# A four-layer decoder trunk on one core: transposes of four head pairs moved from TensorE to VectorE and GpSimd, with edges and one low part reordered

## The chip, the core and the metric

The kernel runs on one core of a Trainium2 chip. A core has five engines that run beside each other: TensorE (PE; its weight loads are listed as PEld), VectorE (DVE), ScalarE (ACT), GpSimd (POOL) and SyncE (SP), which here issues the loads from memory. The metric is the device time of one execution in microseconds, as the median of several runs.

## What is computed

Four layers, each a token mixer and then an MLP with squared ReLU, over one residual stream of 256 tokens by 1024. The mixers are differential attention (layers 0 and 3), block-sparse attention (layer 1, whose one block of 256 makes it plain causal attention here) and sliding-window attention with sinks (layer 2).

```python
for i in range(DEPTH):                       # 4
    a = rms_norm(h, attn_norm_g[i])
    if i % 3 == 0:   y = diff_attention(a, ...)      # 8 heads of 128, (softmax1 - lam * softmax2) v
    elif i % 3 == 1: y = moba_attention(a, ...)      # 16 heads of 64, softmax(q k) v
    else:            y = swa_sink_attention(a, ...)
    h = h + y
    h = h + (max(rms_norm(h, mlp_norm_g[i]) @ w_up, 0) ** 2) @ w_down
return rms_norm(h, final_norm_g)
```

## The kernel before

Every fp32 product is made of two or three faster ones: a matrix is split into a high part, rounded by ScalarE (`whi`, line 188), and a low part, the rest, made by VectorE (`wlo`, line 189). Weights come in pieces of 128x2048 (`raw`, 1 MB each) that SyncE loads up to five pieces ahead of their use (`take`, `FAR`) and that are split two pieces ahead (`LOOK`), each in two halves; the split buffers hold three pieces. A layer uses its pieces in this order: twelve for the input projection (`p_in`), four for the output projection (`p_d`, `p_e` in layer 1), sixteen for the up projection, sixteen for the down projection.

The input projection of layers 0, 1 and 3 makes six groups of 512 columns. For layer 1 they are queries and keys of head pairs 0-1, 2-3, then values, then queries and keys of pairs 4-5 and 6-7, then values. Between the matmuls of these groups stand the attention's steps; a hand-written list, `plan`, says after which group each step is issued: QK (turn queries and keys, `p_qk`, and split them into `qhl` and `kpadh`, `kpadl`), SC (scores `p_s`, then numerators `e`: a mask and row minimum on VectorE, line 466, an exponential on ScalarE, line 469), TR (turn the numerators, `p_t`, and copy them out of PSUM, `et`), AV (product with the values, `p_av`) and, in layers 0 and 3, OUT (turn the results, `p_o`, and split them into `oo`).

In layer 1 a step covers one head pair (two heads of 64, called head 0 to 7 here). `head_block` makes the numerators of both heads in one tile of 128x768, divides them by their sums (line 560) and yields; `next` then runs TR: `transposed` makes six 128x128 transposes on TensorE against an identity (line 131) and two copies by ScalarE (line 485) into one of four `et` tiles, taken in turn; `next` again runs AV: eight matmuls into `p_av`, whose high and low parts go into `oo`. PSUM tiles named "wk" (`p_s`, `p_t`, `p_qk`, `p_av`, `p_o` and others) share four banks in turn.

In layers 0 and 3 `diff_head` combines the two softmaxes (line 518) and `diff_pair` makes the product of two heads, normalises it on VectorE (line 537, tile `o`), and after a `yield` turns it and makes its high part on ScalarE (line 547) and its low part on VectorE (line 548). `ahead` holds one edge that `stage` adds: the first half of one low weight part comes behind line 537 of the last pair.

The order on each engine is made by a scheduler; `TURNS` corrects it on TensorE. Per layer it lists edges such as `(("p_t", 18), ("p_d", 61))`: the matmul number 18 of those that write `p_t` in this layer comes behind number 61 of those that write `p_d`. `behind` makes such an edge between two instructions of one engine; it orders them and waits for nothing. All matmuls have the helper's line 128 in the profile and all transposes line 131, so they are told apart by their tiles.

At the end of the kernel the same way of turning that the change brings into layer 1 exists already for the residual stream: `turn_stream` has VectorE turn squares of 32x32 (line 864) and GpSimd copy them to their places (line 869), in 64 copies of 32x128.

Of the kernel before, what the change touches and what calls it, by code (L numbers as in the profile page):

```python
# [15 lines left out]
OP = mybir.AluOpType  # L16
# [3 lines left out]
P = 128  # L20
# [10 lines left out]
FAR = 5  # L31
WARM = 10
RAW = 4

# [17 lines left out]
        (("p_s", 4), ("p_in", 119)),  # L52
        (("p_s", 42), ("p_d", 41)),
        (("p_d", 150), ("p_d", 161)),
        (("p_o", 12), ("p_d", 126)),
        (("p_t", 18), ("p_d", 61)),
        (("p_av", 18), ("p_t", 23)),
        (("p_av", 21), ("p_d", 84)),
        (("p_s", 7), ("p_in", 116)),
        (("p_s", 12), ("p_in", 164)),  # L60
        (("p_s", 13), ("p_in", 168)),
        (("p_s", 16), ("p_in", 168)),
    ),
    1: (
        (("p_s", 0), ("p_in", 83)),
# [3 lines left out]
        (("p_s", 1), ("p_in", 85)),  # L69
        (("p_s", 13), ("p_in", 133)),  # L70
        (("p_s", 37), ("p_in", 277)),
        (("p_t", 42), ("p_d", 26)),
        (("p_s", 4), ("p_in", 85)),
        (("p_s", 16), ("p_in", 133)),
        (("p_s", 40), ("p_in", 277)),
        (("p_s", 42), ("p_d", 0)),
        (("p_d", 27), ("p_t", 47)),
        (("p_s", 18), ("p_in", 144)),
    ),
    2: (  # L80
# [21 lines left out]
        (("p_s", 4), ("p_in", 85)),  # L102
        (("p_s", 42), ("p_d", 41)),
        (("p_d", 150), ("p_d", 161)),
        (("p_o", 12), ("p_d", 126)),
        (("p_t", 18), ("p_d", 61)),
        (("p_av", 18), ("p_t", 23)),
        (("p_av", 21), ("p_d", 84)),
    ),
}  # L110
# [2 lines left out]
def f(ap):  # L113
    return ap.bitcast(F32)
# [31 lines left out]
def trunk(ctx: ExitStack, tc: tile.TileContext, xT, gains, lams, swa_row, fng, weights, out):  # L146
    nc = tc.nc
    V, A, G, T = nc.vector, nc.scalar, nc.gpsimd, Numbered(nc.tensor)
# [6 lines left out]
    def bank(tag, name):  # L155
        return ps.tile([P, 512], F32, tag=tag, name=name, bufs=4)

    def room(j, shape, name, dt=F32):

        return sb.tile(shape, dt, tag=f"slot{j}", name=name, bufs=1)  # L160


    fetched, staged, highs = [], [], []
# [15 lines left out]
    def stage(w=1024, first=None):  # L179
        i = len(staged)  # L180
        raw = fetched[i]
        hi = sb.tile([P, 2048], F32R, tag="whi", name=f"whi{i}", bufs=LOOK + 1)
        lo = sb.tile([P, 2048], F32R, tag="wlo", name=f"wlo{i}", bufs=LOOK + 1)
        for h in range(2048 // w):
            if first:
                first()
            s = slice(h * w, (h + 1) * w)
            high = A.activation(hi[:, s], raw[:, s], AF.Copy)  # L188
            low = V.tensor_tensor(lo[:, s], raw[:, s], f(hi[:, s]), op=OP.subtract)  # L189
            if (i, h) in ahead:  # L190
                behind(tc, low.ins, ahead[i, h])
        highs.append(high.ins)
        staged.append((hi, lo))

    used = [0]
# [10 lines left out]
    def r3(n):  # L206
        return lambda t: t.rearrange("p (a b) -> p a b", a=n)
# [39 lines left out]
    causal = cst.tile([P, 3, P], F32, name="causal")  # L247
# [193 lines left out]
    scored, turned = [0], [0]  # L441
# [36 lines left out]
    def transposed(es):  # L478
        turned[0] += 1
        ts = room((6, 7, 12, 13)[turned[0] % 4], [P, 2, 3 * P], "et")  # L480
        for i, e in reversed(list(enumerate(es))):
            p = bank("wk", "p_t")
            for j in range(3):
                T.transpose(p[:, P * j:P * j + P], e[:, P * j:P * j + P], ident)
            A.activation(ts[:, i], p[:, :3 * P], AF.Copy)
        return [ts[:, i] for i in range(len(es))]

    def times_v(o, et, v):

        T.matmul(o(0), et[:, 0:P], v(0), start=True, stop=True)  # L490
        T.matmul(o(1), et[:, P:2 * P], v(0), start=True, stop=False)
        T.matmul(o(1), et[:, 2 * P:3 * P], v(1), start=False, stop=True)
# [31 lines left out]
    def diff_pair(slot, ets, v, el, b):  # L524

        p = bank("wk", "p_av")
        for c in range(2):
            times_v(lambda t, c=c: p[:, S * c + P * t:S * c + P * t + P], ets[c], v[c])
        ss = tiny.tile([P, 2 * NT], F32, tag="ss", name="ss")
        for t in range(2 * NT):  # L530
            junk = sb.tile([P, P], F32, tag="junk", name="junk", bufs=1)
            A.activation(junk, p[:, P * t:P * t + P], AF.Square, accum_out=ss[:, t:t + 1])
        V.scalar_tensor_tensor(ss, ss, 1.0 / P, el, op0=OP.mult, op1=OP.add)
        y = tiny.tile([P, 2 * NT], F32, tag="ry", name="ry")
        rsqrt(y, ss, 2 * NT)
        o = sb.tile([P, 2 * NT, P], F32, tag="o", name="o")
        made = V.tensor_tensor(o, p.rearrange("p (t m) -> p t m", m=P), y[:, :, None].to_broadcast([P, 2 * NT, P]),
                               op=OP.mult)
        if b == 6:

            ahead[used[0] + 4, 0] = made.ins
        yield
        p = bank("wk", "p_o")
        for t in range(2 * NT):
            T.transpose(p[:, P * t:P * t + P], o[:, t, :], ident)
        both, gain = part(b, 2), sg[:, slot:slot + 1]
        A.activation(both[:, :, 0], r3(2)(p), AF.Copy, scale=gain)
        V.scalar_tensor_tensor(both[:, :, 1], r3(2)(p), gain, f(both[:, :, 0]), op0=OP.mult, op1=OP.subtract)
        yield [both[:, 0], both[:, 1]]

    def head_block(parts, q, k, v, mask, sinks, b):

        _, both_e, l = scores(q, k, mask, sinks)

        rl = tiny.tile([P, 2, 3], F32, tag="rl3", name="rl3")
        l = l.rearrange("p (c t) -> p c t", c=2)
        V.reciprocal(rl[:, :, 0:2], l)
        V.reciprocal(rl[:, :, 2:3], l[:, :, 1:2])
        e = both_e.rearrange("p c (j m) -> p c j m", j=3)
        V.tensor_tensor(e, e, rl[:, :, :, None].to_broadcast([P, 2, 3, P]), op=OP.mult)  # L560
        es = [both_e[:, c] for c in range(2)]
        yield
        ets = transposed(es)
        yield
        p = bank("wk", "p_av")
        for m, cols in ((0, slice(0, S)), (1, slice(P, S))):
            for c in range(2):
                r = slice(HD * c, HD * c + HD)
                T.matmul(p[r, cols], v(m)[:, r], ets[c][:, S * m:S * m + S - P * m], start=(m == 0), stop=(m == 1),
                         skip_group_check=True)  # L570
        both = part(b)
        A.activation(both[:, 0], p[:, :S], AF.Copy)
        V.tensor_tensor(both[:, 1], p[:, :S], f(both[:, 0]), op=OP.subtract)
        parts.append(both)
# [42 lines left out]
    def mixer_layer(i, n):  # L617
        mixer, slot = i % 3, i // 3
        r = norm_factor(n, i == 0, mixer != 1 and i < 3)
        parts = []  # L620
        kpad = new_keys()
        if mixer == 2:
# [15 lines left out]
            for c in range(4):  # L638
                p = proj(n, (256, 1), False, first)
# [24 lines left out]
        else:  # L664
            v = [room(8 + j, [P, NT, 512], f"v{j}") for j in range(2)]
            vdone = 0
            qk, qs, heads, pairs, ets, els = {}, {}, {}, {}, {}, {}
# [6 lines left out]
            def vh(h):  # L674
                return lambda m: v[h // 4][:, m, P * (h % 4):P * (h % 4) + P]

            def SC(h):
                q, k = [x[:, h % 2] for x in qs[h // 2]], [x[:, h % 2] for x in kpad]
                if mixer == 0:
                    if h % 2 == 0:  # L680
                        els[h // 2] = tiny.tile([P, 2 * NT], F32, tag="el", name="el")
                    heads[h] = diff_head(slot, q, k, els[h // 2][:, NT * (h % 2):NT * (h % 2) + NT])
                else:
                    heads[h] = head_block(parts, q, k, vh(h), causal, None, h)
                next(heads[h])

            def TR(h):
                ets[h] = next(heads[h])

            def AV(h):  # L690
                if mixer:
# [9 lines left out]
            def LAM(_):  # L701
                if i == 0:
                    lambdas()

            order = (0, 1, "v", 2, 3, "v") if mixer else (0, 1, "v", 2, "v", 3)
            plan = [[], [], [(QK, 0), (LAM, 0), (SC, 0)], [(SC, 1)], [(TR, 0), (QK, 1), (SC, 2)], [(TR, 1), (SC, 3)],
                    [(TR, 2)], [(TR, 3)], [(QK, 2), (SC, 4)], [(AV, 0), (AV, 1), (AV, 2), (AV, 3), (SC, 5)],
                    [(TR, 4), (QK, 3), (SC, 6)], [(TR, 5), (SC, 7)],
                    [(TR, 6), (TR, 7), (AV, 4), (AV, 5), (AV, 6), (AV, 7)]]
            if mixer == 0:  # L710
                plan[6:8] = [[(TR, 2), (AV, 0)], [(TR, 3), (AV, 1)]]
# [3 lines left out]
            for at, c in enumerate(order):  # L715
                p = proj(n, (512, 2), at == 0, [lambda do=do, x=x: do(x) for do, x in plan[2 * at]])
# [249 lines left out]
    for i in range(DEPTH):  # L966
        T.layer = i
        parts, rest = mixer_layer(i, n)
# [98 lines left out]
```

## Time and profile before

| | us |
|---|---|
| median of 3 runs | 1133.9 (1132.7 to 1134.74) |
| the profiled execution | 1133.25 |
| its span, first to last instruction | 1131.4 |
| TensorE busy | 1123.7 |
| VectorE busy | 831.9 |
| ScalarE busy | 657.1 |
| GpSimd busy | 56.8 |

A row of the timeline has the start in us from the span's start, the time from the first start to the last end of a run of equal instructions, engine, line, operation, output and inputs, shape, and their number; in brackets stands idle time before it with what ended it. Starts of TensorE's instructions are exact and their ends are modelled, so two neighbouring rows overlap: the distance of their starts is what an instruction cost. In a view by groups the numbers behind the bar are the busy time in us, the mean of one in ns, and the idle time before.

### The profile page before, as it was taken

How to read it: one execution, taken by the hardware profiler on the slowest of the kernel's cores; microseconds unless marked ns; L12 is line 12 of the kernel's file. 1: busy time of each engine (PE TensorE's matmuls, PEld its weight loads, DVE VectorE, ACT ScalarE, POOL GpSimd, SP SyncE). 2: the span in 40 equal slices, each digit the busy share in tenths (PEclk: the TensorE clock that was granted, in tenths of full speed). 3: DMA queues.
4: the chain of work that ended last, by engine and by line, in shares of the span. 5: the costliest groups of instructions: out<-in, count | busy, mean ns of one | idle time of the engine just before them, and what ended most of it. 6: DMA issues, size and time to landing. Idle time of an engine off the chain costs nothing.

```text
span 1131.4 us, 17032 instructions
## 1 busy us (share of the span) xinstructions
PE 1123.7 (99%) x6522; PEld 979.5 (87%) x6522; DVE 831.9 (74%) x1599; ACT 657.1 (58%) x1195; POOL 56.8 (5%) x113
## 2 busy tenths in 40 slices
PE   9999999999999999999999999999999999999997
PEld 7889888888888888888899998888888889888886
DVE  8888977656676698766569888775568788878453
ACT  7766666544476665654446866554446776665342
POOL 2000000000100000000000000000010000002800
PEclk9999999999999999999999999999999999999999
DMA  8643565555544346555563346555554444654551
GB/s 328 203 149 113 178 203 194 196 197 187 171 164 149 115 156 219 193 200 189 196 211 112 113 150 218 191 187 186 186 187 149 150 149 150 213 195 169 186 186 38
DMA packets 30465, 198.66 MB, mean 176 GB/s; under 512 B 3504, under 2 KB 5040, under 8 KB 7216
## 3 DMA queue, kind: packets, MB, share of 16 engines
q1 hardware_dynamic: 30096, 197.09, 50.7%
q8 instruction: 51, 0.84, 0.3%
q10 hardware_dynamic: 288, 0.49, 0.1%
q14 instruction: 30, 0.25, 0.1%
HBM read 196.52 MB, written 1.05 MB: 175 GB/s over the span
## 4 chain that ended last, share of the span: by engine, by line
PE 97%; DMA 1%; issue 0%; SPq 0%; DVE 0%; ACT 0%; POOLq 0%; POOL 0%; DVEq 0%
PE p_up L128 31%; PE p_down L128 24%; PE p_in L128 19%; PE p_last L128 7%; PE p_d L128 7%; PE p_s L128 3%; PE p_av L128 2%; PE p_t L131 1%; PE p_qk L131 1%; DMA raw<-in_weights 1%; PE p_e L128 1%; PE p_o L131 0%; SPq L220 0%; SPq L174 0%; DVE wlo L189 0%
## 5 line engine op out<-in xcount | busy, mean ns | idle before, releaser
L189 DVE TENSOR_TENSOR wlo<-raw,whi 128x1024 fp32r<-128x1024 f32 (+1 forms) x374 | 449.0, 1215 | 187.9 <-ACT whi L188 187.5
L188 ACT ACTIVATE whi<-raw 128x1024 fp32r<-128x1024 f32 (+1 forms) x374 | 383.8, 1045 | 197.7 <-issue 112.9
L128 PE MATMUL p_up<-hg,whi 128*128 128x512 f32 x1024 | 355.3, 394 | 0.0
L128 PE MATMUL p_up<-hg,wlo 128*128 128x256 f32 x1024 | 283.0, 277 | 0.0
L128 PE MATMUL p_down<-uu,whi 128*128 128x512 f32 x768 | 266.4, 394 | 0.0
L128 PEld LDWEIGHTS p_up<-hg,whi 128*128 128x128 f32 x1024 | 191.8, 188 | 44.1
L128 PE MATMUL p_in<-whi,hg 128*128 128x512 f32 (+1 forms) x736 | 212.7, 371 | 0.1
L128 PE MATMUL p_down<-uu,wlo 128*128 128x256 f32 x768 | 212.7, 277 | 0.0
L128 PEld LDWEIGHTS p_up<-hg,wlo 128*128 128x128 f32 x1024 | 192.2, 188 | 0.4
L128 PEld LDWEIGHTS p_down<-uu,whi 128*128 128x128 f32 x768 | 144.0, 188 | 33.5
L128 PEld LDWEIGHTS p_in<-whi,hg 128*128 128x128 f32 x736 | 132.5, 189 | 23.5 <-DVE hg L345 0.8
L128 PEld LDWEIGHTS p_down<-uu,wlo 128*128 128x128 f32 x768 | 144.1, 188 | 0.0
L128 PE MATMUL p_in<-wlo,hg 128*128 128x512 f32 (+1 forms) x368 | 130.1, 368 | 0.3 <-DVE wlo L189 0.3
L834 ACT ACTIVATE uu<-u 128x512 fp32r<-128x512 f32 x64 | 40.5, 632 | 80.4 <-DVE u L832 80.4
L128 PE MATMUL p_d<-oo,whi 128*128 128x256 f32 (+1 forms) x416 | 85.4, 296 | 0.0
L128 PE MATMUL p_last<-whi,uu 128*128 128x512 f32 (+1 forms) x264 | 79.4, 383 | 0.0
L128 PEld LDWEIGHTS p_in<-wlo,hg 128*128 128x128 f32 x368 | 68.8, 189 | 11.6 <-DVE wlo L189 0.8
L754 ACT ACTIVATE cross<-p_up 128x256 f32<-128x256 f32 x128 | 48.0, 375 | 35.5 <-PE p_up L128 34.2
L128 PEld LDWEIGHTS p_d<-oo,whi 128*128 128x128 f32 x416 | 66.5, 190 | 2.1 <-issue 0.2
L344 ACT ACTIVATE hg<-hT,gn 128x256 fp32r<-128x256 f32 x64 | 31.4, 504 | 61.0 <-DVE hT L767 60.9
L469 ACT ACTIVATE e<-ns,nm 128x128 f32<-128x128 f32 (+1 forms) x128 | 56.8, 446 | 13.3 <-DVE nm L466 13.2
L128 PE MATMUL p_d<-oo,wlo 128*128 128x256 f32 x224 | 63.7, 285 | 0.0
(170 smaller groups left out, 1106.3 us busy)
## 6 DMA issues: line engine op xcount, KB each, us to landing
raw<-in_weights SPq DMA_DIRECT2D x181, 1024.0 KB, 4.9
raw<-in_weights SPq DMA_DIRECT2D x8, 256.0 KB, 4.7
raw<-in_weights SPq DMA_DIRECT2D x4, 512.0 KB, 7.6
hT<-in_xT SPq DMA_DIRECT2D x8, 128.0 KB, 4.6
bias<-in_swa_row SPq DMA_DIRECT2D x1, 512.0 KB, 4.4
grow<-in_fng SPq DMA_DIRECT2D x1, 512.0 KB, 3.7
lv<-in_lams SPq DMA_DIRECT2D x1, 256.0 KB, 6.6
out<-given ACTq DMA_DIRECT2D x1, 256.0 KB, 2.7
```

What stands on the lines that cost most here:

```text
L128: return self.keep(out.tensor.name.rstrip("_0123456789"), self.engine.matmul(out, *args, **kw))
L131: return self.keep(out.tensor.name.rstrip("_0123456789"), self.engine.transpose(out, *args, **kw))
L188: high = A.activation(hi[:, s], raw[:, s], AF.Copy)
L189: low = V.tensor_tensor(lo[:, s], raw[:, s], f(hi[:, s]), op=OP.subtract)
L344: A.activation(both[:, 0], h, AF.Copy, scale=g)
L469: A.activation(e[:, s], ns[:, s], AF.Exp, bias=nm[:, t:t + 1], scale=-1.0, accum_out=l[:, t:t + 1])
L754: A.activation(cross, p[:, S:], AF.Copy)
L834: A.activation(both[:, :, 0], r3(2)(u), AF.Copy)
```

## The change

In layer 1 head pairs 0, 1, 2 and 4 (`ASIDE`) no longer use `transposed`. `turned_aside` has VectorE turn every 32x32 square of the 128x768 numerators in one instruction into a new tile (`squares`, in slots 16 and 17, which otherwise serve the end of the kernel), and GpSimd copy the squares to their places in `et`: sixteen copies of 32 partitions by 192 columns for a pair, 64 in all. For pairs 0 to 2 this is issued directly behind the scores; for pair 4 it is moved in `plan` one step forward, behind the products of pairs 0 to 3, whose first `et` tile it takes over.

`lows` keeps the last low half of each weight piece, and the second half of the one that had the edge behind line 537 is now behind the low part of the last results (before line 548), which puts this low part one weight half forward.

In `TURNS` layers 0 and 3 have three edges with other numbers (p_t 18 behind p_d 65 instead of 61; p_av 18 behind p_d 79 instead of p_t 23; p_o 12 behind p_d 125 instead of 126), layer 0 one edge more (p_s 9 behind p_in 115), and layer 1 two edges renumbered for the smaller count of `p_t` and moved: the last pair's transposes come behind p_d 31 instead of 26.

In the built order of instructions this is what moves. On TensorE 24 transposes are gone from layer 1; the scores of pairs 2 and 3 stand together behind matmul 143 and 144 of `p_in` (before, the first stood behind 131 and the second behind 144); the other moves are those of the edges named, four matmuls or fewer each, and in layer 0 matmul p_in 115 stands before p_s 3. On ScalarE eight copies are gone; in layer 1 the second half of the keys for pairs 2 and 3 comes behind two weight roundings; in layers 0 and 3 the copy of head 6 stands between two roundings. On VectorE four turns are added. SyncE's order of loads is the same.

```diff
+ASIDE = (0, 1, 2, 4)
...
-        (("p_o", 12), ("p_d", 126)),
-        (("p_t", 18), ("p_d", 61)),
-        (("p_av", 18), ("p_t", 23)),
+        (("p_o", 12), ("p_d", 125)),
+        (("p_t", 18), ("p_d", 65)),
+        (("p_av", 18), ("p_d", 79)),
...
+        (("p_s", 9), ("p_in", 115)),
...
-        (("p_t", 42), ("p_d", 26)),
+        (("p_t", 18), ("p_d", 31)),
...
-        (("p_d", 27), ("p_t", 47)),
+        (("p_d", 32), ("p_t", 23)),
...
         highs.append(high.ins)
+        lows.append(low.ins)
...
+    def turned_aside(pair_e, h):
+
+        turned[0] += 1
+        ts = room((6, 7, 12, 13)[turned[0] % 4], [P, 2, 3 * P], "et")
+        z = room(16 + h % 2, [P, 2, 3 * P], "squares")
+        V.transpose(z.rearrange("p c m -> p (c m)"), pair_e.rearrange("p c m -> p (c m)"))
+        to, at = (x.rearrange("p c (j i m) -> p (c j) i m", j=3, m=32) for x in (ts, z))
+        for g in range(4):
+            for i in range(4):
+                G.tensor_copy(to[32 * i:32 * i + 32, :, g, :], at[32 * g:32 * g + 32, :, i, :])
+        return [ts[:, i] for i in range(2)]
...
-            ahead[used[0] + 4, 0] = made.ins
+            then = used[0] + 4
+            ahead[then, 0] = made.ins
...
-        V.scalar_tensor_tensor(both[:, :, 1], r3(2)(p), gain, f(both[:, :, 0]), op0=OP.mult, op1=OP.subtract)
+        made = V.scalar_tensor_tensor(both[:, :, 1], r3(2)(p), gain, f(both[:, :, 0]), op0=OP.mult, op1=OP.subtract)
+        if b == 6:
+            behind(tc, lows[then], made.ins)
...
-    def head_block(parts, q, k, v, mask, sinks, b):
+    def head_block(parts, q, k, v, mask, sinks, b, aside=False):
...
-        ets = transposed(es)
+        ets = turned_aside(both_e, b) if aside else transposed(es)
...
-                    heads[h] = head_block(parts, q, k, vh(h), causal, None, h)
+                    heads[h] = head_block(parts, q, k, vh(h), causal, None, h, h in ASIDE)
                 next(heads[h])
+                if mixer and h in ASIDE and h < 4:
+                    next(heads[h])
 
             def TR(h):
-                ets[h] = next(heads[h])
+                if not (mixer and h in ASIDE and h < 4):
+                    ets[h] = next(heads[h])
...
-                    [(TR, 2)], [(TR, 3)], [(QK, 2), (SC, 4)], [(AV, 0), (AV, 1), (AV, 2), (AV, 3), (SC, 5)],
-                    [(TR, 4), (QK, 3), (SC, 6)], [(TR, 5), (SC, 7)],
+                    [(TR, 2)], [(TR, 3)], [(QK, 2), (SC, 4)], [(AV, 0), (AV, 1), (AV, 2), (AV, 3), (TR, 4), (SC, 5)],
+                    [(QK, 3), (SC, 6)], [(TR, 5), (SC, 7)],
```

More of the change, by code (lines that the diff above doesn't have):

```diff
@@ L104 @@
         (("p_d", 150), ("p_d", 161)),
-        (("p_o", 12), ("p_d", 126)),
-        (("p_t", 18), ("p_d", 61)),
-        (("p_av", 18), ("p_t", 23)),
+        (("p_o", 12), ("p_d", 125)),
+        (("p_t", 18), ("p_d", 65)),
+        (("p_av", 18), ("p_d", 79)),
         (("p_av", 21), ("p_d", 84)),
@@ L160, in room @@
         return sb.tile(shape, dt, tag=f"slot{j}", name=name, bufs=1)
-    fetched, staged, highs = [], [], []
+    fetched, staged, highs, lows = [], [], [], []
     ahead = {}
```

## The prediction

> **What bounds the kernel now.** I read the page first, then busy time by stretch, then TensorE's timeline where the change touches it, and last the timelines of the engines that feed it.
>
> ```profile
> span 1131.4 us, 17032 instructions
> PE 1123.7 (99%) x6522; PEld 979.5 (87%) x6522; DVE 831.9 (74%) x1599; ACT 657.1 (58%) x1195; POOL 56.8 (5%) x113
> ...
> PE 97%; DMA 1%; issue 0%; SPq 0%; DVE 0%; ACT 0%; POOLq 0%; POOL 0%; DVEq 0%
> ...
> 327.00:400.00 73.00, 72.87 (x424) 61.05 (x423) 51.83 (x123) 51.63 (x117) 0.00 (x0) 1.00 0.42 145
> ```
>
> TensorE (PE) works 99% of the span, and 97% of the chain of waits is its own. The last row is the attention of the second layer (layer 1) (columns: PE, PEld, DVE, ACT, POOL, clock, DMA share, GB/s): PE 72.87 of 73 us, VectorE (DVE) 51.8, ScalarE (ACT) 51.6, GpSimd (POOL) nothing, clock 1.00, DMA at 0.42. So the time is the sum of what TensorE issues plus its short stalls. What leaves TensorE is won, unless its replacement arrives late; what is put on VectorE and GpSimd costs nothing until TensorE waits for it. "Busy" hides short stalls, since a matmul's end is modelled; I find them as the distance between starts against the usual step (0.228 us for 512 columns, 0.12 for 256, 0.11 for a transpose).
>
> **The change part by part.** *Transposes taken from TensorE.* Heads 0, 1, 2 and 4 of the second layer (each a pair) lose six transposes each.
>
> ```profile
> 327.02 0.82 PE L131 MATMUL p_t<-ident,e 128*128 128x128 f32 x6
> 327.67 1.04 PE L131 MATMUL p_qk<-ident,qk 128*128 128x128 f32 x8
> ...
> 361.98 2.82 PE L128 MATMUL p_av<-et,v 128*64 128x256 f32 x32
> ```
>
> Six transposes hold the next instruction back 327.67 - 327.02 = 0.65 us. Four such blocks go: 4 x 0.65 = **-2.60 us**. Eight copies out of PSUM leave ScalarE too, which wins nothing by itself.
>
> *The last pair's transposes.* In the built order they stand three output-projection matmuls later.
>
> ```profile
> 386.10 0.96 DVE L560 TENSOR_TENSOR e<-e,rl 128x768 f32<-128x768 f32 x1
> ...
> 386.80 0.28 PE L128 MATMUL p_d<-oo,wlo 128*128 128x256 f32 x1
> 387.21 0.85 PE L131 MATMUL p_t<-ident,e 128*128 128x128 f32 x6
> 387.99 2.82 PE L128 MATMUL p_av<-et,v 128*64 128x256 f32 x32
> ```
>
> From 386.80 to 387.21 are 0.41 us where a step is 0.12: 0.29 us of waiting for the numerators, ready at 387.06. The chain that makes them starts from TensorE's scores, so it moves forward with TensorE; three more matmuls (0.12 + 0.23 + 0.12 = 0.47 us) cover the hole: **-0.29**.
>
> *Edges in the first and the fourth layer (layers 0 and 3).*
>
> ```profile
> 100.15 0.75 DVE L518 SCALAR_TENSOR_TENSOR e<-e,c 128x128 f32<-128x128 f32 x2
> ...
> 100.26 0.40 PE L128 MATMUL p_d<-oo,whi 128*128 128x256 f32 x2
> 100.65 0.74 PE L131 MATMUL p_t<-ident,e 128*128 128x128 f32 x3
> 101.35 0.40 PE L128 MATMUL p_d<-oo,whi 128*128 128x256 f32 x2
> ...
> 930.35 0.40 PE L128 MATMUL p_d<-oo,whi 128*128 128x256 f32 x2
> ...
> 931.42 0.40 PE L128 MATMUL p_d<-oo,whi 128*128 128x256 f32 x2
> ```
>
> From 100.26 to 101.35 are 1.09 us for three matmuls and three transposes (3 x 0.12 + 3 x 0.11 = 0.69): 0.40 lost, waiting for the numerators that VectorE ends at 100.90; in the fourth layer 1.07 - 0.69 = 0.38. Four matmuls (0.48 us) now stand ahead, so the transposes come at 100.98: **-0.40 and -0.38**. The copy of this result on ScalarE now stands between two weight roundings, and the product that reads it (p_av 18) is moved behind four matmuls.
>
> ```profile
> 101.74 0.48 ACT L485 ACTIVATE et<-p_t 128x384 f32<-128x384 f32 x1
> 102.11 2.00 ACT L188 ACTIVATE whi<-raw 128x1024 fp32r<-128x1024 f32 x2
> ...
> 103.22 0.83 PE L128 MATMUL p_av<-v,et 128*128 128x128 f32 x6
> ```
>
> One rounding of 1.0 us from 101.74 and the copy behind it end at 103.2; the product comes at 103.22 - 0.40 + 0.48 = 103.3: 0.1 us to spare, no cost.
>
> ```profile
> 110.29 2.35 DVE L189 TENSOR_TENSOR wlo<-raw,whi 128x1024 fp32r<-128x1024 f32 x2
> 112.56 0.74 DVE L548 SCALAR_TENSOR_TENSOR oo<-p_o,gn,oo 128x512 fp32r<-128x512 f32 x1
> ...
> 113.15 0.59 PE L128 MATMUL p_d<-oo,whi 128*128 128x256 f32 x2
> 113.58 0.28 PE L128 MATMUL p_d<-oo,wlo 128*128 128x256 f32 x1
> ...
> 943.22 0.58 PE L128 MATMUL p_d<-oo,whi 128*128 128x256 f32 x2
> 943.64 0.28 PE L128 MATMUL p_d<-oo,wlo 128*128 128x256 f32 x1
> ```
>
> The low part of the last results (L548) waits behind two 1.2 us weight operations and ends at 113.30; the matmuls there take 0.43 and 0.42 us for two steps of 0.12: 0.19 and 0.18 us of stall. With one weight operation moved behind it, and its transposes one matmul earlier, it ends over 0.5 us sooner: **-0.19 and -0.18**. The weight half behind it is for the up projection, which reads it several microseconds later.
>
> ```profile
> 34.52 0.69 DVE L615 TENSOR_TENSOR kpadl<-p_qk,kpadh 64x512 fp32r<-64x512 f32 x1
> ...
> 34.84 0.40 PE L128 MATMUL p_in<-whi,hg 128*128 128x512 f32 x1
> 35.35 0.47 PE L128 MATMUL p_s<-kpadh,qhl 128*128 128x512 f32 x1
> ```
>
> The new edge in the first layer puts one ready 512-column matmul (p_in 115) into the hole before 35.35, where TensorE waits 0.28 us for the keys: **-0.23**.
>
> *What the new road costs.* Four VectorE turns of 128x768, 64 GpSimd copies of 32x192.
>
> ```profile
> 323.27 0.95 DVE L560 TENSOR_TENSOR e<-e,rl 128x768 f32<-128x768 f32 x1
> ...
> 364.43 0.96 DVE L560 TENSOR_TENSOR e<-e,rl 128x768 f32<-128x768 f32 x1
> ...
> 1042.75 1.29 DVE L864 STREAM_TRANSPOSE squares<-hT 128x512 f32<-128x512 f32 x2
> ...
> L869 POOL COPY res<-squares x64: 279/288/1360, 1039.6 to 1072.2; 32x128 f32<-32x128 f32 x64
> 1039.64 33.74 POOL L869 COPY res<-squares 32x128 f32<-32x128 f32 x64 [80.37 <-DVE squares L864]
> ...
> L189 DVE TENSOR_TENSOR wlo<-raw,whi x11: 1216/1221/1226, 324.7 to 359.4; 128x1024 fp32r<-128x1024 f32 x11
> L189 DVE TENSOR_TENSOR wlo<-raw,whi x14: 1185/1276/1314, 1039.4 to 1073.1; 128x1024 fp32r<-128x1024 f32 x14
> ...
> L235 POOL MEMSET ones<- 128x128 f32 x1 | 0.2, 204 | 0.3 <-POOLq L1056 0.3
> L250 POOL MEMSET causal<- 128x384 f32 x1 | 0.4, 422 | 0.0
> ```
>
> A turn: 0.64 us for 512 columns, so about 0.96 for 768 (L560 has the same shape and takes 0.95). VectorE is idle for 21 of the 73 us; weights are split two pieces ahead; four turns stay hidden. A copy of 32x128 takes 0.288 us undisturbed and, with its issue, 0.33; up to 1.36 when VectorE runs a weight split beside it, and the split grows from 1221 to 1276 ns. For 192 columns: not below 0.33, not above 1.5 x 0.33 = 0.49; the memsets grow by 0.85 ns a column, so I take 0.33 + 0.055 = 0.385.
>
> Are they in time? Head 0's turn ends near 325.3 (behind L560 at 323.27 and a mask operation). The first product to read the copies is the block at 361.98, by then 3 x 0.65 = 1.95 earlier, and head 2's part lies 1.4 us inside: 361.4. That leaves 36.1 us for 48 copies, **0.75 us each**. In this time VectorE does twelve splits, three normalisations and one rotation of two SBUF inputs, some 12 x 1.22 + 3 x 0.95 + 1.4 = 19 us; free are 17 us, or 44 copies at 0.385, and as in the older stretch about one slips in at each of the blocking operations (19 more): 63 places for 48. At 0.49 it is 35 + 19 = 54. Head 4's sixteen have from about 365 to 385, 1.2 us each. So: hidden, and if the cover fails the product block waits one for one.
>
> The thin place is the scores of heads 2 and 3, which now stand together behind the "v" projection: the second half of the keys is rounded only after both halves of a weight piece on ScalarE.
>
> ```profile
> 331.49 2.01 ACT L188 ACTIVATE whi<-raw 128x1024 fp32r<-128x1024 f32 x2 [0.40 <-PE p_in L128]
> ...
> 335.10 0.82 PE L131 MATMUL p_t<-ident,e 128*128 128x128 f32 x6
> ```
>
> That piece starts 0.65 earlier, at 330.84, and ends at 332.85, the keys at about 333.4; TensorE reaches the scores at 335.10 - 0.65 - 1.04 (six score matmuls moved behind) = 333.4. The keys' low half follows in much the same way. No slack: between 0 and 0.9 us lost (three VectorE operations each held 0.29 us by a copy); I take **+0.2**, nearer the 0.055 us that a split was seen to lose.
>
> **Sum**: -2.60 - 0.29 - 0.78 - 0.37 - 0.23 + 0.20 = -4.07 us. The profiled execution took 1133.25 us (1131.4 span and 1.85 around it): 1129.2. The runs' median of 1133.9 lies 0.65 above that execution; I add half of it: **1129.5 us**. What can be told from no change is 0.2%, 2.3 us.
>
> A rule of the Trainium skill speaks against the change: "SBUF — State Buffer", section "SBUF: two separate sides", says that VectorE with two SBUF inputs and GpSimd share one port pair as an exclusive lock, held for a whole instruction, the other blocking fully. The blocked copies agree (up to 1.36 us), while the splits lost 0.055 us where a whole copy would be 0.29. By the rule alone about 19 VectorE operations would lose 0.29 to 0.34 us each, 6 us on VectorE, and the time would be the next rival's.
>
> **The rivals.** (a) *VectorE is held by the copies*: each two-input operation between 325 and 361 loses a whole copy. For it: the lengthened splits; against: by 0.055, not 0.29. Price where it meets TensorE, the scores of heads 2 and 3: 0.9 instead of 0.2, and as much again at the numerators of head 3: 1129.5 + 1.4 = 1130.9. (b) *Only the transposes win*: each closed hole opens again behind (the copy on ScalarE comes late at p_av 18, the keys at 35.35): 1129.5 + 1.67 - 0.2 = 1131.0. (c) *Slower: the product block at 362 waits for head 2's copies.* It decides from a mean of 0.75 us a copy; the win is gone at 36.1 + 4.1 = 40.2 us, 0.84 each, and it is slower by over 0.2% from 0.89. At 0.95 the block starts 45.6 - 36.1 = 9.5 us late: 1139. For it: the older 64 copies took 33.74/64 = 0.53 each, and half as much again would be 0.79 (1.8 us late, 1131.3); against: only a copy's column part grows. (d) *No change*: copies late by about what is won, 1133.
>
> **How the numbers follow.** Forecast 0.64 (its own range 1128.3 to 1130.6), (a) 0.12, (b) 0.08, (d) 0.07, (c) 0.09. Faster than 1131.6: the first three less a little, 0.80; within 0.2%: (d) and edges of (b) and (c), 0.10; slower: 0.10. The range 1128.2 to 1132.2 leaves out (c), (d) and a little below.
>
> **What would show it.** Right: 24 fewer p_t matmuls; no hole before the transposes at 100, 387 and 930 (shifted); GpSimd's copies ending near 355 and again before 380, 0.4 to 0.6 us each; the 32 products at about 360 without a wait. Wrong: a TensorE or PEld wait on POOL "et" at the product block; a hole over 0.5 us at the scores near 333; weight splits over 1.3 us; a new hole at 103 or 35.

## The result and the profile after

| kernel | median of its 20 runs, us | range | ratio |
|---|---|---|---|
| before | 1133.22 | 1132.63 to 1134.74 | |
| changed | 1132.64 | 1128.91 to 1133.47 | 0.9984 [0.9977, 0.9990] |

The change gains 0.16%, less than the 0.2% that the prediction set as the bound of what can be told from no change. Behind the median stand two groups with nothing between them: 7 runs of the changed kernel lie at 1128.9 to 1130.1 us (median 1129.5), 13 at 1132.5 to 1133.5. The profile was taken in a run of the upper group (1132.64 us). The mean granted clock of the single runs is 0.998 to 1.000 in both groups, so the clock doesn't part them.

First the parts that the prediction named. The page of the changed kernel, its view of `p_t`, and its timeline on GpSimd and on TensorE around the product block and the scores of pairs 2 and 3:

```profile
span 1130.9 us, 17053 instructions
PE 1123.8 (99%) x6498; PEld 978.9 (87%) x6498; DVE 836.2 (74%) x1603; ACT 654.2 (58%) x1187; POOL 92.7 (8%) x177
```

```profile
L133 PE MATMUL p_t<-ident,e x120: 270/272/295, 42.2 to 932.7; 128*128 128x128 f32 x120
```

```profile
324.32 29.95 POOL L500 COPY et<-squares 32x192 f32<-32x192 f32 x48 [18.84 <-DVE squares L496]
365.00 8.52 POOL L500 COPY et<-squares 32x192 f32<-32x192 f32 x16 [10.73 <-DVE squares L496]
...
332.06 0.39 PE L130 MATMUL p_in<-whi,hg 128*128 128x512 f32 x1
332.44 0.62 PE L130 MATMUL p_s<-kpadh,qhl 128*128 128x256 f32 x2
...
358.92 0.39 PE L130 MATMUL p_in<-whi,hg 128*128 128x512 f32 x1
359.24 2.82 PE L130 MATMUL p_av<-et,v 128*64 128x256 f32 x32
```

There are 120 transposes instead of 144. GpSimd's 48 copies take 0.62 us each on the average and end at 354.27, 5.0 us ahead of the product block, whose 32 products run without a wait. Between 332.06 and 332.44 lies a hole of 0.16 us (the distance is 0.39; the same pair of forms at 332.91 costs 0.23), the one at the scores that the prediction allowed for. So the mechanism is the one forecast. VectorE's two pieces of it by lines and by tile, and the 48 copies by tile (min/median/max ns behind the count):

```profile
L496 DVE STREAM_TRANSPOSE squares<-e 128x768 f32<-128x768 f32 x4 | 3.9, 968 | 0.0
```

```profile
L191 DVE TENSOR_TENSOR wlo<-raw,whi x10: 1218/1280/1362, 324.5 to 349.6; 128x1024 fp32r<-128x1024 f32 x10
```

```profile
L500 POOL COPY et<-squares x48: 333/343/1382, 324.3 to 353.9; 32x192 f32<-32x192 f32 x48
```

A turn is 0.97 us (forecast 0.96). The average of the copies hides two kinds: 33 of the 48 take 0.33 to 0.35 us and two 0.44, and 13 take 0.98 to 1.38. Each of the 13 ends 0.20 to 0.21 us behind the end of a weight split or of a normalisation (L578) that runs beside it, as if it had stood still until then. VectorE loses less: a weight split 0.06 us at the median and 0.14 at most against the 1221 ns of before, never a whole copy of 0.34.

Now what was not forecast. Two stages of layer 1 behind its attention (`p_e`, then `p_down`; the first and the last start stand behind the three durations), of before and of after:

```profile
L128 PE MATMUL p_e<-oo,whi x32: 391/391/391, 396.9 to 407.6; 128*128 128x512 f32 x32
...
L128 PE MATMUL p_down<-uu,whi x256: 392/394/395, 496.8 to 585.2; 128*128 128x512 f32 x128
```

```profile
L130 PE MATMUL p_e<-oo,whi x32: 395/398/403, 393.2 to 404.2; 128*128 128x512 f32 x32
...
L130 PE MATMUL p_down<-uu,whi x256: 395/398/403, 494.9 to 585.0; 128*128 128x512 f32 x128
...
L130 PE MATMUL p_down<-uu,whi x256: 392/394/395, 207.0 to 295.4; 128*128 128x512 f32 x128
```

At `p_e` the changed kernel leads by 3.7 us, at the last `p_down` of the layer by 0.2. Each of these 256 pairs (a 512-column matmul with the high part, a 256-column one with the low part) took 88.4/255 = 346.7 ns before and 90.1/255 = 353.3 ns after; the last row is the changed kernel's own layer 0, at 346.7. No row in this stretch shows idle time, the granted clock is 1.00 in both. Close up, from the timelines of after and of before:

```profile
450.06 0.40 PE L130 MATMUL p_up<-hg,whi 128*128 128x512 f32 x1
450.30 0.28 PE L130 MATMUL p_up<-hg,wlo 128*128 128x256 f32 x1
450.41 0.40 PE L130 MATMUL p_up<-hg,whi 128*128 128x512 f32 x1
450.64 0.28 PE L130 MATMUL p_up<-hg,wlo 128*128 128x256 f32 x1
450.76 0.40 PE L130 MATMUL p_up<-hg,whi 128*128 128x512 f32 x1
451.00 0.28 PE L130 MATMUL p_up<-hg,wlo 128*128 128x256 f32 x1
451.12 0.40 PE L130 MATMUL p_up<-hg,whi 128*128 128x512 f32 x1
```

```profile
450.00 0.40 PE L128 MATMUL p_up<-hg,whi 128*128 128x512 f32 x1
...
450.35 0.39 PE L128 MATMUL p_up<-hg,whi 128*128 128x512 f32 x1
...
450.69 0.40 PE L128 MATMUL p_up<-hg,whi 128*128 128x512 f32 x1
...
451.04 0.39 PE L128 MATMUL p_up<-hg,whi 128*128 128x512 f32 x1
```

Three pairs are 1.06 us after and 1.04 before. The records hold starts to the nanosecond; the distances from each start to the next, H the 512-column matmul and L the 256-column one, are

```
before, p_up of layer 1:  H231 L113 H232 L118   and again       (two pairs, 694 ns)
after,  p_up of layer 1:  H241 L120 H236 L113 H233 L117  again  (three pairs, 1060 ns)
```

Both are cycles that keep themselves up. I call them the two-pair and the three-pair cycle. Ahead of its first `p_up` the kernel before runs evenly, with distances of 230 and 117, at the same 346.7 ns a pair as in the two-pair cycle. From 410 to 585 us there are some 500 pairs, at 6.6 ns each 3.3 us: the distance of the two groups, and most of the 3.5 us that the profile gives back from the first `p_e` on. The differences of the starts of the same matmul, after less before, are -1.0 us at the end of layer 0, -3.4 at the first `p_up` of layer 1, -0.2 at the first `p_in` of layer 2, and -0.6 at the end.

### The profile page after: what moved, and what is told of

It is laid out like the page before. It is cut to its first block, busy times and chain, and to the rows that moved or that the text cites. A ratio compares the mean times of both kernels' runs of the same rounds, so it can differ in the third digit from the quotient of the medians.

```text
span 1130.9 us, 17053 instructions
## 1 busy us (share of the span) xinstructions
PE 1123.8 (99%) x6498; PEld 978.9 (87%) x6498; DVE 836.2 (74%) x1603; ACT 654.2 (58%) x1187; POOL 92.7 (8%) x177
## 4 chain that ended last, share of the span: by engine, by line
PE 97%; DVE 1%; issue 1%; DMA 0%; SPq 0%; ACT 0%; POOLq 0%; POOL 0%; DVEq 0%
PE p_up L130 32%; PE p_down L130 24%; PE p_in L130 19%; PE p_last L130 7%; PE p_d L130 7%; PE p_s L130 3%; PE p_av L130 2%; PE p_t L133 1%; PE p_qk L133 1%; PE p_e L130 1%; DMA raw<-in_weights 0%; PE p_o L133 0%; DVE wlo L191 0%; DVE hg L348 0%; DVE acc L357 0%
```

## The experiments

What can change the cycle? Two places in layer 1 stand out in the order of TensorE. One is the resumption after the last pair's block of transposes and products, with p_d 27 (an L) before, with p_d 32 (an H) after. The other is the first `p_up` group, where the code itself puts `h7 h8 l7 h9 l8 l9` in place of `h l h l h l` (I call it the first swap); in layer 1 alone the scheduler makes a second such swap nine pairs on, because the last four matmuls of that group wait for VectorE's last normed row and are put behind the start of the next group. In the profile after, the first swap falls on the 236 of the cycle; in layers 0, 2 and 3 of both kernels it falls on the 241 and the stream behind it is in the two-pair cycle.

The kernel before was run beside each set; its own runs turned out to have an upper group too: 0 of 20 in the first comparison, then 13 of 18 (1136.2 to 1137.2), 6 of 29 and 7 of 23. The three sets (e1 to e4, e5 to e8, e9 to e12) ran on three chips, and before's share of upper runs differs between them, so shares of different sets are compared with care. In what follows groups are compared, not medians. Only the changed kernel has a profile of each group; no profile is of the upper group of before, e4, e5 or e9.

| kernel | runs of the lower group | of the upper |
|---|---|---|
| changed | 7 (1128.9 to 1130.1) | 13 (1132.5 to 1133.5) |
| e1, resumes with L | 5 (1129.6 to 1131.1) | 0 |
| e2, resumes two pairs earlier | 2 (1129.6, 1130.6) | 5 (1133.0 to 1133.5) |
| e3, first swap one pair earlier in all layers | 5 (1140.8 to 1141.5), one group | |
| e4, before, block one matmul earlier | 11 (1133.2 to 1134.0) | 1 (1136.6) |
| e5, e1 without the second swap | 6 (1129.1 to 1130.2) | 6 (1132.7 to 1133.5) |
| e6, changed, without the second swap | 0 | 12 (1132.4 to 1133.8) |
| e7, e6 with layer 1's first swap one pair earlier | 6 (1129.3 to 1130.8) | 0 |
| e8, before, without the second swap | 12 (1132.9 to 1134.3) | 0 |
| e9, e7 with no pair turned aside | 9 (1131.5 to 1132.9) | 3 (1134.9 to 1135.9) |

**e1, resuming with an L.**

```diff
-        (("p_t", 18), ("p_d", 31)),
+        (("p_t", 18), ("p_d", 30)),
...
-        (("p_d", 32), ("p_t", 23)),
+        (("p_d", 31), ("p_t", 23)),
```

> The changed kernel with the last pair's block (transposes 18 to 23 and its products) one matmul earlier: after p_d 30 in place of p_d 31, so that TensorE resumes with p_d 31, a low-part matmul (128x256), and not with p_d 32, a high-part one (128x512). Theory (cycle): TensorE's stream of alternating 128x512 and 128x256 matmuls can run in a cycle of two pairs (before: 346.7 ns a pair) or of three (after, 388 to 585 us: 241+120, 236+113, 233+117 = 353.3 ns a pair), and which of them follows is settled by how it resumes after the block and by where in the three-pair cycle the order h7 h8 l7 of the first p_up group falls. Resumed with a low part, as before, it runs at 346.7 ns throughout: every run near 1129.5, none in the upper group of 1132.5 to 1133.5. Rival (VectorE's turns, GpSimd's copies or the missing transposes disturb the stage): two groups of runs as in the changed kernel, some 13 in 20 at 1133. Rival (chance alone): the same.

All five runs in the lower group, ratio 0.9949 [0.9937, 0.9961] (against runs of before that were mostly in its upper group, so the ratio flatters). The rows of `p_down`, and the second swap in the timeline, both of e1:

```profile
L130 PE MATMUL p_down<-uu,whi x256: 392/394/395, 493.6 to 582.0; 128*128 128x512 f32 x128
```

```profile
410.29 0.71 PE L130 MATMUL p_up<-hg,whi 128*128 128x512 f32 x2
410.83 0.28 PE L130 MATMUL p_up<-hg,wlo 128*128 128x256 f32 x1
```

88.4 us for 255 pairs: 346.7 ns, with GpSimd's copies and VectorE's turns all in place. The second swap costs 0.54 us for two H steps where 0.46 is usual: TensorE comes to it earlier here and waits some 0.08 us for the last normed row. So e1 left open whether the resumption or that wait keeps the 346.7 ns; e5 was to tell.

**e2, the block two pairs earlier** (p_t 18 behind p_d 27, p_d 28 behind p_t 23).

> The changed kernel with the same block two pairs earlier: after p_d 27, TensorE resumes with p_d 28, again a high part. From there to the order h7 h8 l7 are 2+16+32+7 = 57 pairs in place of 55, so that h7 falls on the 241 ns place of the three-pair cycle, where it falls in layers 0, 2 and 3, and the stream there goes back to two pairs. Theory (cycle): 353.3 ns at most up to 408 us, 57 pairs x 6.6 ns = 0.4 us, then 346.7: 1129.5 to 1130.2 in every run (the block could wait up to 0.3 us for its numerators). Rival (only the kind of the matmul that it resumes with counts): most runs at 1132.5 to 1133.5. Rival (GpSimd, VectorE): the same two groups.

Missed: five of seven runs in the upper group. The trace shows why. The stream was in the three-pair cycle up to the first swap, which fell on the 241 as computed, and it was in the two-pair cycle behind it (231, 112, 233, 117); six pairs on, the second swap, passed without a wait, put it back, and `p_down` runs at 353.3 ns. The first place behaves as expected; I had overlooked the second.

**e3, the first swap one pair earlier, in every layer.**

```diff
-                steps[7:10] = [(order[7 + x], w) for x, w in ((0, "h"), (1, "h"), (0, "l"), (2, "h"), (1, "l"), (2, "l"))]
+                steps[6:9] = [(order[6 + x], w) for x, w in ((0, "h"), (1, "h"), (0, "l"), (2, "h"), (1, "l"), (2, "l"))]
```

> The changed kernel with its edges as they are; only the order h7 h8 l7 h9 l8 l9 in the first p_up group of each layer stands one pair earlier (h6 h7 l6 h8 l7 l8). In layer 1 it then comes after 54 pairs in place of 55, on the 241 ns place. Theory (cycle): layer 1 goes back to 346.7 ns a pair at 407 us, 54 pairs x 6.6 ns = 0.4 us lost: 1129.9 for layer 1 alone. In layers 0, 2 and 3 the same shift puts it off the 241 ns place, which leaves them at 353.3 ns: each about 480 pairs x 6.6 ns = 3.2 us, up to 9.5 us in all, 1139. So layer 1 is to be read by itself in the profile: 346.7 there, 353.3 in the others. Rival (GpSimd, VectorE, chance): layer 1 stays at 353.3 in most runs, the others at 346.7, time as that of the changed kernel.

The kernel becomes 8.4 us slower than the changed one (1141.07 us, ratio to before 1.0044 [1.0032, 1.0056]) by a matmul's place in the order. `p_down` of e3 in layer 0 and in layer 1:

```profile
L130 PE MATMUL p_down<-uu,whi x256: 395/398/403, 209.0 to 299.1; 128*128 128x512 f32 x128
...
L130 PE MATMUL p_down<-uu,whi x256: 395/398/403, 498.7 to 588.8; 128*128 128x512 f32 x128
```

Layer 0 is at 90.1/255 = 353.3 ns, and so are layers 2 and 3: the three-pair cycle where no head is turned aside and nothing else differs from the changed kernel. In layer 1 the stream went back to two pairs at the first swap and was put out again at the second, as in e2; the expectation for layer 1 was wrong for that reason.

**e4, the kernel before with its block one matmul earlier** (p_t 42 behind p_d 25, p_d 26 behind p_t 47).

> The kernel before, with its last pair's block one matmul earlier in layer 1: after p_d 25 in place of p_d 26, so that it resumes with p_d 26, a high part, 3+16+32+7 = 58 pairs ahead of h7, which is the place in the three-pair cycle of the changed kernel (58 and 55 leave the same rest by 3). No VectorE turn and no GpSimd copy is in it. Theory (cycle): layer 1 runs at 353.3 ns a pair from 388 to 585 us in some or all runs, +3.3 us: those at 1136.5, the others at 1133.3. Rival (GpSimd, VectorE, missing transposes): 1133.3 in every run, at most 0.2 us more for a longer wait ahead of the block.

One run of twelve in the upper group. It doesn't test what it was built for: the scheduler put another swap right behind the resumption (distances H335 L119 L119 H236), and the stream came to `p_e` in the two-pair cycle. Its profile shows one thing more: the first swap put it into the three-pair cycle, and a wait of 0.04 us at the second took it out again.

**e5 and e6, no second swap.** Two more edges put the whole end of the first `p_up` group behind a pair of the next: e5 is e1 with them, e6 the changed kernel with them.

```diff
         (("p_s", 18), ("p_in", 144)),
+        (("p_up", 28), ("p_up", 37)),
+        (("p_up", 30), ("p_up", 37)),
```

> The changed kernel resuming with the low part p_d 31 (as e1) and, in layer 1, with two more edges that put the last four matmuls of the first p_up group (p_up 28 to 31) behind a whole pair of the second group (p_up 37), so that the second h h l h l l of layer 1 (at 410 us in e1, where TensorE also waited 0.08 us for the last normed row's low part) is gone. Theory (cycle, two places): e1 was fast in 5 of 5 because it resumed in the two-pair cycle and the wait at that second place kept it there. Without the second place nothing can push it out: 346.7 ns a pair from 388 to 585 us, every run 1129.4 to 1131, the wait of 0.08 us gone or smaller. Rival (only the wait holds the fast cycle): without it a part of the runs goes to 1133. Rival (GpSimd, VectorE): two groups.

> The changed kernel with these two edges and nothing else: it resumes with the high part p_d 32, h7 of the first swap falls on the 236 ns place (where the profile of the changed kernel stayed in the three-pair cycle), and no second swap and no wait is left that could bring it back. Theory (cycle, two places): all or nearly all runs at 353.3 ns a pair, 1132.5 to 1133.5; the 7 in 20 at 1129.5 of the changed kernel came from a short wait at the second place and are gone. Rival (the second swap is what makes it slow): every run at 1129.5. Rival (which cycle it resumes in is chance): 7 in 20 at 1129.5 as before.

e6 came as the theory has it: with the resumption in H and no second swap, 12 of 12 runs are in the upper group, where the changed kernel had 13 of 20. e5 didn't: 6 of 12 in the upper group. Its profile is one of the lower, with 346.7 ns throughout. So, if e5's upper runs are in the three-pair cycle as well, resuming with an L isn't enough by itself. That the wait at the second swap helped e1 is likely, not shown: with 11 of 17 runs of the two kernels in the lower group, five of five for e1 would come by chance about once in 13, and the two ran on different chips.

**e7, e6 with the first swap one pair earlier in layer 1 alone.**

```diff
-                steps[7:10] = [(order[7 + x], w) for x, w in ((0, "h"), (1, "h"), (0, "l"), (2, "h"), (1, "l"), (2, "l"))]
+                at = 6 if T.layer == 1 else 7
+                steps[at:at + 3] = [(order[at + x], w) for x, w in ((0, "h"), (1, "h"), (0, "l"), (2, "h"), (1, "l"), (2, "l"))]
```

> As e6, and in layer 1 alone the first swap one pair earlier (h6 h7 l6), which puts it after 54 pairs, on the 241 ns place, where e3 and e2 went back to two pairs. Theory (cycle, two places): 353.3 ns from 388 to 407 us (0.4 us lost), then 346.7 to 585 us with nothing behind it that undoes it, the other layers at 346.7: 1129.4 to 1130.5 in every run. One pair's place in the order is then all that differs from e6, for 3 us. Rival (chance, GpSimd, VectorE): the same spread of runs as e6.

Six of six in the lower group, median 1129.49 us, ratio to before 0.9955 [0.9938, 0.9973]. The first swap in the timelines of e6 and of e7, and `p_e` and `p_down` of e7:

```profile
407.30 0.63 PE L132 MATMUL p_up<-hg,whi 128*128 128x512 f32 x2
407.77 0.28 PE L132 MATMUL p_up<-hg,wlo 128*128 128x256 f32 x1
```

```profile
406.80 0.64 PE L132 MATMUL p_up<-hg,whi 128*128 128x512 f32 x2
407.28 0.28 PE L132 MATMUL p_up<-hg,wlo 128*128 128x256 f32 x1
```

```profile
L132 PE MATMUL p_e<-oo,whi x32: 394/398/404, 393.4 to 404.3; 128*128 128x512 f32 x32
...
L132 PE MATMUL p_down<-uu,whi x256: 391/394/396, 493.5 to 581.9; 128*128 128x512 f32 x128
```

The two H steps are 0.47 us in e6 (236 and 228 ns) and 0.48 in e7 (241 and 236). `p_e` is at 353 ns a pair, `p_down` at 346.7. One pair's place decides 3.5 us (the medians of e6 and e7), and every run of e7 is faster than every run of before and than the changed kernel's upper group.

**e8, the kernel before without the second swap.**

> The kernel before with the same two edges in layer 1 (the last four matmuls of the first p_up group behind p_up 37). On the last chip its own runs fell in two groups, 5 near 1133.5 and 13 near 1136.6. It resumes with a low part (p_d 27). Theory (cycle, two places): it comes to the second swap at 346.7 ns a pair, and the second swap, when the wait of 0.08 us there is missing, sends it into the three-pair cycle: without the swap every run is near 1133.2, none at 1136.5. Rival (the two groups come from elsewhere): a part of the runs stays at 1136.5.

Twelve of twelve in the lower group, beside 6 of 29 of the unchanged kernel before in the upper. That fits the expectation and doesn't prove it; with these counts twelve of twelve would come by chance about once in 16 ((23/29) to the twelfth).

**e9, e7 with no pair turned aside** (`ASIDE = ()`, the block's edges with the old numbers of `p_t` at the same place, p_t 42 behind p_d 31 and p_d 32 behind p_t 47).

> e7 with no head turned aside: all eight pairs of layer 1 again turned by TensorE (24 transposes more, no squares, no GpSimd copies), the last pair's block at the same place between the products of the first projection (p_t 42 to 47 behind p_d 31), so that 54 pairs still lie between it and the first swap. What is left of the change are its moved edges and the low part turned first. Theory of the prediction: the 24 transposes are worth 2.60 us, the wait of 0.27 us at the scores of the third and fourth pair goes with the copies: 1129.5 + 2.60 - 0.27 = 1131.8, all runs in one group. Rival (the copies or VectorE's turns cost TensorE time that the trace does not show): nearer to 1131 or below. Rival (the edges alone had made the gain): 1129.5.

The lower group has its median at 1131.8, 2.3 us over e7: the gain of the copies as forecast (2.60 - 0.27 = 2.33). `p_e` of e9 in its profile, a run of the lower group:

```profile
L132 PE MATMUL p_e<-oo,whi x32: 395/398/403, 395.4 to 406.4; 128*128 128x512 f32 x32
```

Without any turn on VectorE or copy on GpSimd, TensorE resumes with p_d 32 in the three-pair cycle here too (353 ns a pair), so these turns and copies don't bring the cycle about. Three runs of twelve lie 3.3 us higher, which the theory didn't expect of this order; no profile is of them.

**e10, pair 2's copies made twice, on e7.**

```diff
-                G.tensor_copy(to[32 * i:32 * i + 32, :, g, :], at[32 * g:32 * g + 32, :, i, :])
+                for _ in range(2 if h == 2 else 1):
+                    G.tensor_copy(to[32 * i:32 * i + 32, :, g, :], at[32 * g:32 * g + 32, :, i, :])
```

> e7 with the 16 GpSimd copies of head pair 2 made twice (the same values to the same place). In e7 the 48 copies run from 324.44 to 354.37 us at 0.62 us each, and the block of 32 products begins at 359.06 us, those of pair 2 half of 2.82 us later, near 360.5. With 64 copies they end at 324.44 + 64 x 0.62 = 364.3 us. Theory (the prediction's slower rival, its place and slack): TensorE waits some 3.8 us ahead of the products of pair 2, 1129.5 + 3.8 = 1133.3 (3.3 to 5.3 more, the upper end if the scheduler puts the wait ahead of the whole block). If the copies had more room than the trace shows (TensorE's order or the scheduler moves the block): under 1 us more.

GpSimd and TensorE in its timeline, and its windows (the columns are busy us and counts of PE, PEld, DVE, ACT and POOL, then the granted clock, the DMA share and GB/s):

```profile
326.26 38.79 POOL L503 COPY et<-squares 32x192 f32<-32x192 f32 x64 [18.93 <-DVE squares L498]
...
361.19 1.52 PE L132 MATMUL p_av<-et,v 128*64 128x256 f32 x16
365.10 2.83 PE L132 MATMUL p_av<-et,v 128*64 128x256 f32 x16 [2.40 <-POOL et L503]
```

```profile
360.00:365.10 5.10, 2.71 (x22) 1.71 (x20) 5.03 (x16) 2.59 (x9) 4.63 (x9) 0.98 0.59 199
365.10:368.00 2.90, 2.90 (x17) 1.81 (x17) 0.83 (x3) 1.30 (x3) 0.00 (x0) 0.50 0.03 11
```

The block waits for pair 2 where the prediction's slower rival placed it. Between the last matmul ahead of the block and the first behind it e10 loses 3.9 us against e7 (6.99 us between the two starts, 3.07 in e7): 2.40 of waiting, and most of the rest because the granted clock is 0.50 in the 2.9 us behind the wait, where sixteen products take 2.83 us that are half of 2.82 otherwise. The expectation had 3.8 us of waiting alone, so that the sum comes near it is luck: the wait was shorter and its cost larger than one for one, which the prediction had assumed. The Trainium skill ("TensorE: Matmul & The Clock Gate", section "What's actually happening") has TensorE at half clock after an idle window of about 3.4 us; here 2.40 us were enough. The runs spread more than others (1131.6 to 1136.6, median 1134.15), the profiled one partly by 1.7 us of waits for the first loads.

**e11 and e12, the kernels of e5 and of the change once more**, for a profile of the other group.

> e5 unchanged, once more, since its runs fell in two groups (6 near 1129.5, 6 near 1133) and its profile was one of the first group. If this profile is of the second group: theory (cycle) has layer 1 at 353.3 ns a pair from a place that the trace names, either from the resumption at 387 us or from the first swap at 408 us on, with every other stage as in e5. Rival: the 3.3 us lie elsewhere, as a wait or in another layer.

> The changed kernel unchanged, once more, for a profile of its group near 1129.5 (7 of 20 so far). If this is one: theory (cycle) has layer 1 at 346.7 ns a pair up to 585 us, with a wait at the second swap near 410 us or a resumption at 387 us in the two-pair cycle, and every other stage as in its first profile. If it is of the group near 1133: as the first profile, 353.3 ns.

e11 took 1129.15 us, again the lower group, so e5's upper group has no profile. e12 took 1130.6 us: the lower group, though its TensorE leaves the waits for the first weights near 19 us 1.2 us later than in the first profile. `p_e` and `p_down` of e12, and the second swap in the timelines of e12 and of the changed kernel's first profile:

```profile
L130 PE MATMUL p_e<-oo,whi x32: 395/398/403, 394.5 to 405.5; 128*128 128x512 f32 x32
...
L130 PE MATMUL p_down<-uu,whi x256: 391/391/391, 494.7 to 583.1; 128*128 128x512 f32 x128
```

```profile
411.48 0.63 PE L130 MATMUL p_up<-hg,whi 128*128 128x512 f32 x2
411.95 0.28 PE L130 MATMUL p_up<-hg,wlo 128*128 128x256 f32 x1
```

```profile
410.15 0.62 PE L130 MATMUL p_up<-hg,whi 128*128 128x512 f32 x2
410.61 0.28 PE L130 MATMUL p_up<-hg,wlo 128*128 128x256 f32 x1
```

Both executions resume in the three-pair cycle (`p_e` 353 ns) and pass the first swap in it. At the second the two H steps take 0.47 us in e12 (236 and 233 ns) and 0.46 in the first profile (235 and 226), and from there e12 runs at 346.7 ns a pair and the other does not. With eight nanoseconds over 3 us are won.

## Why the prediction was right and wrong

*The transposes and the hole at the last pair's block (-2.60, -0.29) and the loss at the scores (+0.20)*: right. The starts of e7 against those of before move by 2.33 us from the start of the layer's attention (-0.95) to its first `p_up` (-3.28), and by the 0.32 us that e7 loses in the three-pair cycle up to there (48 pairs at 6.6 ns): 2.65, forecast 2.69. e9 gives the copies' part alone, 2.3.

*Layers 0 and 3*: right. The transposes' hole, the low part and what is given back between them come to -0.51 us in layer 0 (forecast -0.59) and -0.51 in layer 3 (forecast -0.56), by the same comparison. The edge at 35 us: -0.21, forecast -0.23.

*The copies*: right. The average of 0.62 us isn't the price that the prediction put at 0.385: an undisturbed copy took 0.34, and from start to start 0.38. The rest is the blocking that it counted apart, one copy held at each two-input operation of VectorE. Its 63 places in 36.1 us would be 27.5 us for 48 copies; they took 29.95, under the deadline of 36.1, and e10 showed that the deadline is real. Rival (a), a whole copy lost by each such VectorE operation, isn't in the rows: 0.06 us at the median.

*The sum*: -4.07 forecast; where the two-pair cycle holds, -3.7 between the lower groups (1133.2 to 1129.5) and -3.82 between the matmuls of the profiles of before and e7. The predicted 1129.5 us is the median of the changed kernel's lower group, and to the tenth this is luck: the forecast started from 1133.6, 0.35 us above before's median of 1133.22 in twenty runs, and its gain was 0.35 us too large.

The median of all runs, 1132.64 us, lies 0.44 above the range of 1128.2 to 1132.2, and the gain is 0.6 us where 4.07 were summed. As a share of before it stands just at the range's edge (0.9984 against 1132.2/1133.9 = 0.9985), but only because the three runs of before that the forecast had lay 0.7 us above the twenty: luck, not the mechanism.

*What failed* is the step "How the numbers follow": it took the duration of everything the change doesn't touch over from the profile of before, and gave the case of no change 0.07 with "copies late by about what is won" as its only way. The time came out at 1132.64 because 13 of 20 runs gave 3.3 us back in projections that the change doesn't touch: moving the block to p_d 32 had TensorE resume in a cycle of 353.3 instead of 346.7 ns a pair, and the profile of such a run stays in it past the second swap, up to 585 us. All eight profiles that resume with an H and go on in the plain order (after, e2, e3, e6, e7, e9, e10, e12) have `p_e` at 353 ns a pair, and all five that resume with an L (before, e1, e5, e8, e11) at 346.7. Of the forecast's "wrong" signs only splits over 1.3 us were there (1.36 at most), and nothing waited for them; no wait and no hole of the size named. The sign was a pair of matmuls 2% longer, five hundred times. That the cycle is what cost it is shown by e6 and e7 (0 of 12 against 6 of 6 in the lower group, in one set, one pair's place apart), by e12 (the same kernel with 346.7 ns in `p_down` and 3.2 us less from the second swap on), and by e3, which brings the three-pair cycle into layers 0, 2 and 3. e9 shows that it is the block's place and not the copies that sets the cycle at the resumption.

*Still open*: what in TensorE makes the cycles; what puts half of e5's runs and three of e9's in the upper group, since no profile caught one; and what makes the eight nanoseconds of e12. In both executions the first weight load within the second swap starts 0.054 us behind the end of VectorE's last normed row, some 0.08 us behind the start of the swap where 0.003 is usual, so both seem to wait for that row there, and the wait alone doesn't part them.

## What to carry to other kernels

When a change wins at its place and the total doesn't show it, compare the start of the same matmul in both traces along the whole span: a wait shows as a step, a change of pace as a slope. A stream of alternating matmuls can have more than one steady pace, so a reordering is to be judged by the spacing behind it as well, and by the single runs, not only by their median. Where such a stream is upset, look at the few places where its order breaks (a block in between, a swap, a short wait) before looking at the other engines.

## What the runs showed of the hardware

- Alternating 128x512 and 128x256 matmuls with a weight load each ran at 346.7 or at 353.3 ns a pair, for 500 pairs on end, at a granted clock of 1.00 and without a wait in the records. An order break (two 512-column steps in a row) can move the stream from the one to the other (e7 and e2), and so did a wait of 0.04 us at such a break (e4); one of 0.08 us left it at 346.7 ns (e1).
- GpSimd's copy of 32x192 took 0.33 to 0.35 us undisturbed; 13 of 48 took 0.98 to 1.38 us, and each of these ended 0.2 us behind a VectorE operation with two SBUF inputs that ran beside it. VectorE's splits of 1.22 us lost 0.06 at the median. Of the rule of the Trainium skill that the prediction weighed, "SBUF — State Buffer", section "SBUF: two separate sides", with the other engine blocked for a whole instruction, the copies fit the one half (GpSimd blocked by VectorE); the other half, VectorE blocked for a whole copy, isn't what its rows show here.
- A wait of 2.40 us on TensorE was followed by a granted clock of 0.50 for the next 2.9 us (e10).
